# A batched matmul on one core: half of the last group's x moved to GpSimd's DMA queue

## The chip, the cores and the metric

The kernel runs on one core of a Trainium2 chip. The core has five engines with an instruction stream each (TensorE or PE, VectorE or DVE, ScalarE or ACT, GpSimd or POOL, SyncE or SP) and sixteen DMA engines that they share. The metric is the device time of one execution in microseconds (us), lower is better. A run of the kernel before took 517.88 us (median of three, 517.79 to 517.91).

## What is computed

```python
def setup_inputs():
    b1, b2, m, k, n = 8, 16, 256, 512, 384
    return {
        "x": np.random.randn(b1, b2, m, k).astype(np.float32),
        "weight": np.random.randn(b1, b2, k, n).astype(np.float32),
    }

def reference(x, weight):
    return np.matmul(x, weight).astype(np.float32)
```

These are 128 products of a 256x512 by a 512x384 matrix: x has 67.1 MB, weight 100.7 MB, the output 50.3 MB, 218 MB in all, each moved once.

## The kernel before

**Tiling.** The 128 batches are taken in NG = 32 groups of G = 4. One group has 1024 rows of x. They lie in SBUF as 128 partitions of R = 8 rows, 16 KB for a partition, 2 MB in all. Its w has 3 MB, its output 1.5 MB. In groups 0 to 30 a partition holds eight consecutive rows of x, so a partition belongs to one batch, and the multiplication is done with 32 columns at a time for each batch. In the last group, n = 31 (`is_full`, L123), x is laid out by batch instead: a partition holds two consecutive rows of each of the four batches, four runs of 4 KB, and each batch is multiplied at the full width of 128 (`multiply_full`, L251).

**Stages.** For each group, x is loaded as float32 (`load_x`, L108), cast to bf16 by DVE in T = 4 pieces of two rows (`cast_x`, L164; the line of the copy in the profile is L171), transposed by PE in pairs of bf16 taken as float32 words (`transpose`, L216, L224), copied out of PSUM by ACT (`evacuate`, L205, L211) and multiplied (`multiply`, L231, L242; the last group L260). w is loaded (`load_w`, L126), cast to bf16 by DVE and ACT (`cast_w`, L176, L184), or by DVE alone in the first four and the last two groups (`cast_short`, L189, L200), for which w also comes in two halves with a semaphore each (`h_in`). ACT copies the products from PSUM to SBUF (`copy_out`, L269, L275), and they are stored (`store`, L142, L157). In the last group, piece q of x, of its cast and of its product is batch q of the four.

**Buffers and order.** x and w have two buffers each (XS, WS), the output four. The order on each engine is written out by hand, and semaphores count the pieces. Every load and store is issued by SyncE, which runs through them in the order x of n + 4, store of n, w of n + 4, and waits in front of each until its buffer is free or its data are there. For x of group n that is `x_cast` reaching (n - 1) * 4, that is, the cast of group n - 2 wholly done (L111): group 29 for group 31. Since SyncE waits in order, a load stands behind the wait of the one before it. Its last issues are: x of 30, store of 26, w of 30 in halves, x of 31, w of 31 in halves, the stores of groups 27 to 30, and the store of 31, in a layout by batch as its x (L145, L154). Then SyncE waits for the stores, with a short loop and some semaphore increments between (L305 to L310).

**DVE's order** in a step n is: cast w of group n, cast x of group n + 1 (`next_x`, L315). In the last steps this makes: w of 29, x of 30, w of 29 (rest), w of 30, x of 31, w of 31. `cast_x` waits for the load once, ahead of its first piece (L166, L167).

**GpSimd** makes the identity matrix for the transposes at the start (`on_gpsimd`, L280) and has no further work until the closing barrier.

**DMA semaphores.** A transfer adds 16 to its semaphore. The trace has sixteen increments of one for every transfer, each at its own time, one for each DMA engine.

## Time and profile before

| | us |
|---|---|
| median of three runs | 517.88 |
| the profiled execution | 517.57 |
| its span in the profile | 515.80 |
| PE busy (matmul) | 320.0 (62%) |
| DVE busy | 397.7 (77%) |
| ACT busy | 409.7 (79%) |
| POOL busy | 0.7 |

The span runs from the first to the last instruction; the execution is 1.77 us longer. 218.18 MB were moved at a mean of 423 GB/s. The parts of the profile used here are: the page with its forty equal slices (a digit is a busy share in tenths), the table of stretches (busy time of each engine, granted clock, mean busy share of the sixteen DMA engines, GB/s), the chain of work that ended last (start, duration, what), and the timeline (start, duration, engine, line, operation, out<-in, and in brackets how long the engine stood idle before it and for whom).

SyncE's last issues, from the timeline: w of 30 at 464.46 (both halves, 0.80 us), x of 31 at 465.32 (0.42 us), w of 31 at 480.32 (0.81 us), the stores from 481.23 on, the last at 506.13. From issue to landing, x took 22.3 us in the median, a store 25.0 us, a half of w 16.7 us.

### The profile page before, as it was taken

The page shows a single profiled execution, that of the slowest core. Times are in us where ns is not written, and L with a number is a line of the kernel's source. Part 1 is how long each engine was busy: PE and PEld are TensorE (multiplying, and loading weights), DVE is VectorE, ACT ScalarE, POOL GpSimd, SP SyncE. Part 2 cuts the span into 40 slices and gives each one's busy share as a digit, 9 for nine tenths or more (in the row PEclk, how much of TensorE's full clock was granted, in tenths as well). Part 3 has the DMA queues.
Part 4 walks back from the last instruction along what each step waited for, and adds up shares of the span by engine and source line. Part 5 has one row for each costly group of instructions (what it writes and reads, how often), then busy time and mean ns, then how long its engine had stood idle before and what let it go on. Part 6 is the DMA issues. An engine that isn't in the chain of part 4 may idle for free.

```text
span 515.8 us, 11659 instructions
## 1 busy us (share of the span) xinstructions
PE 320.0 (62%) x4512; PEld 222.0 (43%) x4512; DVE 397.7 (77%) x462; ACT 409.7 (79%) x387; POOL 0.7 (0%) x6
## 2 busy tenths in 40 slices
PE   2276737567586656675655864767657477656871
PEld 2254425444354443453443543535445354434550
DVE  2788757788777897777977778877789777797960
ACT  1365577798978997987998799889798978997751
POOL 0000000000000000000000000000000000000000
PEclk9698878677866877876888686778667876877697
DMA  8999999999999999999999999999999999999996
GB/s 337 428 423 426 437 430 420 435 431 433 431 424 432 430 439 428 429 426 432 433 436 428 423 434 431 437 429 425 430 431 434 433 429 427 430 435 423 421 429 250
DMA packets 15462, 218.18 MB, mean 423 GB/s; under 512 B 1632, under 2 KB 1632, under 8 KB 2656
## 3 DMA queue, kind: packets, MB, share of 16 engines
q1 hardware_dynamic: 15456, 218.11, 99.3%
q8 instruction: 3, 0.05, 0.0%
q14 instruction: 3, 0.02, 0.0%
HBM read 167.77 MB, written 50.33 MB: 423 GB/s over the span
## 4 chain that ended last, share of the span: by engine, by line
DMA 57%; DVE 29%; issue 9%; PE 1%; DVEq 1%; SPq 1%; ACT 0%; POOLq 0%
DMA w_sb<-in_weight_dram 57%; DVE w_bf L184 20%; DVE x_bf L171 5%; DVE w_bf L200 4%; PE po L260 1%; SPq L135 0%; DVEq L334 0%; SPq L118 0%; DVEq L62 0%; DVEq L180 0%; ACT out_sb L275 0%; SPq L130 0%; DVEq L168 0%; DVEq L194 0%; SPq L422 0%
## 5 line engine op out<-in xcount | busy, mean ns | idle before, releaser
L184 DVE CAST w_bf<-w_sb 32x1536 bf16<-32x1536 f32 x286 | 271.9, 951 | 81.1 <-DMA w_sb<-in_weight_dram 73.0
L242 PE MATMUL po<-w_bf,x_t 128*32 128x384 bf16 x3968 | 201.5, 364 | 33.4 <-DVE w_bf L184 25.4
L224 PE MATMUL pt<-identity,x_bf 128*128 128x128 f32 x512 | 113.5, 409 | 149.1 <-DVE x_bf L171 149.1
L184 ACT CAST w_bf<-w_sb 32x1536 bf16<-32x1536 f32 x130 | 191.0, 1470 | 5.1 <-DMA w_sb<-in_weight_dram 1.9
L224 PEld LDWEIGHTS pt<-identity,x_bf 128*128 128x128 f32 x512 | 101.3, 223 | 161.5 <-issue 161.0
L242 PEld LDWEIGHTS po<-w_bf,x_t 128*32 128x32 bf16 x3968 | 117.7, 107 | 116.3 <-issue 51.5
L275 ACT COPY out_sb<-po 128x768 f32 (+1 forms) x128 | 102.5, 800 | 59.7 <-PE po L242 53.9
L211 ACT COPY x_t<-pt 128x1024 bf16<-128x1024 bf16 x128 | 123.6, 1021 | 20.9 <-PE pt L224 20.3
L171 DVE CAST x_bf<-x_sb 128x1024 bf16<-128x1024 f32 x128 | 80.0, 688 | 12.5 <-DMA x_sb<-in_x_dram 11.7
L200 DVE CAST w_bf<-w_sb 64x1536 bf16<-64x1536 f32 x48 | 45.8, 955 | 8.3 <-DMA w_sb<-in_weight_dram 7.0
L211 ACT ACT_TABLE_LOAD x1 | 1.3, 1283 | 10.8 <-PE pt L224 10.8
L260 PE MATMUL po<-w_bf,x_t 128*128 128x384 bf16 x32 | 5.4, 326 | 2.8 <-DVE w_bf L200 2.8
L260 PEld LDWEIGHTS po<-w_bf,x_t 128*128 128x128 bf16 x32 | 3.1, 98 | 5.1 <-issue 3.1
masks.py:199 POOL TENSOR_SCALAR_AFFINE_SELECT identity<-identity 128x128 f32<-128x128 f32 x1 | 0.3, 294 | 0.2 <-POOL identity L281 0.2
L281 POOL MEMSET identity<- 128x128 f32 x1 | 0.2, 205 | 0.5 <-POOLq L62 0.5
L411 POOL MEMSET const-bfloat16-1.0<- 128x1 bf16 x1 | 0.1, 102 | 0.0
L411 POOL MEMSET const-uint8-127<- 128x1 uint8 x1 | 0.1, 102 | 0.0
L411 POOL MEMSET const-float32-0.0<- 128x1 f32 x1 | 0.1, 99 | 0.2 <-issue 0.2
L411 POOL MEMSET const-float32-1.0<- 128x1 f32 x1 | 0.1, 99 | 0.0
## 6 DMA issues: line engine op xcount, KB each, us to landing
w_sb<-in_weight_dram SPq DMA_DIRECT2D x26, 3072.0 KB, 18.2
x_sb<-in_x_dram SPq DMA_DIRECT2D x32, 2048.0 KB, 22.3
out_dram<-out_sb SPq DMA_DIRECT2D x32, 1536.0 KB, 25.0
w_sb<-in_weight_dram SPq DMA_DIRECT2D x12, 1536.0 KB, 16.7
```

What stands on the lines that cost most here:

```text
L171: e.tensor_copy(out=x_bf[s % BS][:, rows].rearrange("p r (s q c) -> p r s q c", s=S, c=KO), in_=x_sb[s % XS][:, rows].rearrange("p r (q s ...
L184: copy(out=w_bf[(s * G + i) % WBS][h * C : (h + 1) * C], in_=w_sb[s % WS][i * C : (i + 1) * C, h * KO : (h + 1) * KO, :],).then_inc(w_vcas ...
L200: e.tensor_copy(out=w_bf[(n * G + d * SH + a) % WBS][h * p : (h + 1) * p], in_=w_sb[n % WS][a * p : (a + 1) * p, r : r + KO, :],).then_inc ...
L211: e.copy(out=x_t[s % TS][:, 2 * q : 2 * q + 2], in_=pt[(s * T + q) % PT][:].bitcast(bf16),).then_inc(t_copied, 1)
L224: ins = e.transpose(pt[(s * T + q) % PT][:, rr, h, :], words[:, 2 * q + rr, h :: KO // 2], identity[:],)
L242: ins = e.matmul(po[(s * T + q) % PO][mine, rr, :N], x_t[s % TS][:, 2 * q + rr, ko // 2, mine, ko % 2], w_bf[(s * G + i) % WBS][:, ko, :], ...
L260: ins = e.matmul(po[(s * T + q) % PO][:, rr, :N], x_t[s % TS][:, 2 * q + rr, ko // 2, :, ko % 2], w_bf[(s * G + q) % WBS][:, ko, :], start ...
L275: e.copy(out=out_sb[:, bass.ds(slot(t, U, s) * R + 2 * q, 2), :], in_=po[(s * T + q) % PO][:, :, :N],).then_inc(o_copied, 1)
L281: e.memset(identity[:], 0.0).then_inc(id_done, 1)
L411: nc = _bacc.Bacc("TRN2", target_bir_lowering=False, num_devices=1)
```

## The change

GpSimd gets a function `load_rest`. After the identity it waits for the same count of `x_cast` that SyncE waits for ahead of x of group 31, resets the cursor of its DMA descriptors, and issues the loads of batches 2 and 3 of that group (the pieces `G // 2 :` of each partition, two runs of 4 KB, 1 MB in all) as three transfers of 5, 121 and 2 partitions, on a semaphore of their own (`rest_in`). SyncE's load of group 31 is cut to batches 0 and 1, 1 MB, at its old place. DVE's cast of that group waits for `rest_in` to reach 48 ahead of its third piece (q = 2), the first that reads the other half.

```diff
+    rest_in = sems("rest_in", 1)[0]
...
         rows = x_rows[bass.ds(n * (G * M), G * M)]
         if is_full(n):
-            src = rows.rearrange("(i p r) k -> p i r k", i=G, p=P)
-            dst = x_sb[s % XS][:].rearrange("p (i r) k -> p i r k", i=G)
+            src, dst = (v[:, : G // 2] for v in full_x())
         else:
             src, dst = rows.rearrange("(p r) k -> p r k", r=R), x_sb[s % XS][:]
         e.dma_start(dst, src).then_inc(x_in[s % XS], 16)
+
+    def full_x():
+        n = NG - 1
+        src = x_rows[n * G * M : (n + 1) * G * M].rearrange("(i p r) k -> p i r k", i=G, p=P)
+        return src, x_sb[n % XS][:].rearrange("p (i r) k -> p i r k", i=G)
+
+    def load_rest(e):
+        n = NG - 1
+        e.wait_ge(x_cast, n * T + (1 - XS) * T)
+        e.inc_swdge_sem([], [], mode="reset_dge_cursor")
+        src, dst = full_x()
+        p = 0
+        for k in (5, 121, 2):
+            e.dma_start(dst[p : p + k, G // 2 :], src[p : p + k, G // 2 :]).then_inc(rest_in, 16)
+            p += k
...
         if q == 0:
             e.wait_ge(x_in[s % XS], (t * (U // XS) + s // XS) * 16 + 16)
+        if q == T // 2 and is_full(n):
+            e.wait_ge(rest_in, 16 * 3)
         e.wait_ge(t_made, n * T + (q + 1 - T + BIAS))
...
         e.drain().then_inc(id_done, 1)
+        load_rest(e)
```

## The prediction

> **What bounds the kernel now.** I read the transfers' view first, since the page has DVE at 77% and ACT at 79% of the span and PE at 62%, and none of them full. Page, slices and queues:

> ```profile
> DMA  8999999999999999999999999999999999999996
> ...
> GB/s 337 428 423 426 437 430 420 435 431 433 431 424 432 430 439 428 429 426 432 433 436 428 423 434 431 437 429 425 430 431 434 433 429 427 430 435 423 421 429 250
> ...
> q1 hardware_dynamic: 15456, 218.11, 99.3%
> ```

> Only the first and last slice fall below 420 GB/s. The sixteen DMA engines are the bound, all on SyncE's queue, and transfers wait in it: the last x was issued at 465.32 and landed at 487.99. So time can only come from the two ends. The end, by stretches of 1 us (last two columns: mean busy share of the sixteen, GB/s):

> ```profile
> 506.00:507.00 1.00, 0.00 (x0) 0.00 (x0) 0.00 (x0) 0.11 (x1) 0.00 (x0) 1.00 0.50 209
> 507.00:508.00 1.00, 0.00 (x0) 0.00 (x0) 0.00 (x0) 0.00 (x0) 0.00 (x0) 1.00 0.97 393
> ...
> 511.00:512.00 1.00, 0.00 (x0) 0.00 (x0) 0.00 (x0) 0.00 (x0) 0.00 (x0) 0.50 0.23 89
> 512.00:513.00 1.00, 0.00 (x0) 0.00 (x0) 0.00 (x0) 0.00 (x0) 0.00 (x0) 0.50 0.07 28
> 513.00:514.00 1.00, 0.00 (x0) 0.00 (x0) 0.00 (x0) 0.00 (x0) 0.00 (x0) 0.50 0.07 27
> ```

> 0.07 is one engine in sixteen (0.0625): from 512.2 on a single DMA engine works, and in 506:507 half of them have nothing to do. They end unequally. The records of each transfer's sixteen semaphore increments, one for each DMA engine, say by how much (us behind the first, 11th to 16th; the records are in order of time and don't name the engine):

> ```
> transfer, landed      11th  12th  13th  14th  15th  16th
> first w,      12.42   0.37  0.38  0.43  0.55  0.66  0.73
> next w half,  17.23   0.37  0.41  0.54  0.65  0.71  1.84
> w, group 3,   50.41   0.53  0.64  0.72  1.63  1.69  1.90
> w, second to last half, 491.69   1.03 1.33 1.89 1.98 2.45 3.60
> w, last half, 495.36  1.01  1.32  1.87  1.95  2.42  3.58
> store of 30, 510.46   1.02  1.33  1.91  1.99  2.44  4.11
> store of 31, 514.54   0.12  0.19  0.63  0.73  1.17  3.22
> ```

> Eleven lie within 1.02 us, five straggle by up to 4.1. The stragglers are made partly by instruction fetches: three packets of 16 KB on the instruction queue (15.2, 35.0 and 43.5 us, about 1.03 to 1.1 us each) precede the three steps of about 1 us in the table.

> The chain of waits breaks off at the last ACT copy. Its last lines, with SyncE's and DVE's:

> ```profile
> 480.32 11.37 DMA w_sb<-in_weight_dram
> ...
> 499.91 5.37 PE po L260 x32
> 505.29 0.02 issue
> 505.31 0.80 ACT out_sb L275
> ```

> ```profile
> 458.99 2.50 DVE L171 CAST x_bf<-x_sb 128x1024 bf16<-128x1024 f32 x4
> 461.52 2.91 DVE L184 CAST w_bf<-w_sb 32x1536 bf16<-32x1536 f32 x3
> 466.99 7.83 DVE L184 CAST w_bf<-w_sb 32x1536 bf16<-32x1536 f32 x8 [2.55 <-DMA w_sb<-in_weight_dram]
> ...
> 488.21 2.50 DVE L171 CAST x_bf<-x_sb 128x1024 bf16<-128x1024 f32 x4
> 491.81 7.86 DVE L200 CAST w_bf<-w_sb 64x1536 bf16<-64x1536 f32 x8 [1.09 <-DMA w_sb<-in_weight_dram]
> ```

> The last store is issued at 506.13 and its engines without backlog finish together near 511.35: that is the floor which the compute chain sets, 5.2 us after the issue. The end, 514.54, lies 3.2 us above it, on one DMA engine which was still busy with store 30. So the end is backlog of the slowest DMA engine, not the chain.

> **The change, part by part.** *Prices.* x of group 31 goes in packets of 4 KB, four for a partition: between the landings of the w before it (482.92) and its own (487.99) lie 5.07 us for 8 partitions per engine, 0.158 us a packet and 0.317 us for a partition's half. Store 31 takes an engine that starts late 3.70 us (13th to 15th: 508.26 to 511.95, 508.34 to 512.05, 508.79 to 512.49); the 16th took 4.08, with an 8 KB instruction packet of 0.31 us at 513.79 behind its data.

> *SyncE.* Its one x issue (0.42 us) stays, at half the bytes; nothing leaves its queue.

> *GpSimd.* One wait, one cursor reset, three issues, none of them in the trace of before. The wait is met when the casts of group 29 end, 461.49, which is 3.8 us ahead of SyncE's issue, and these packets needn't stand behind SyncE's backlog. Behind them on POOL stands only the closing barrier (from 499.75). The cost of an issue is bounded below by SyncE's 0.33 us, above by a whole landing time, 22.7 us; I take the low end, SyncE's issue being the nearest row, so about 1.3 us for the four, and with the 0.9 us from issue to first packet seen at store 31 (506.13 to 507.06) the rest starts near 464. The third cast of x, which now waits for it, starts at 489.46. At any price up to about 20 us this is hidden under DVE's work until then; without that cover each us goes onto DVE's chain. Starting early gains nothing by itself: the DMA share is 0.98 at 460 to 464, so early bytes displace others.

> *DVE.* One more semaphore check, 0.05 us by the like step at 491.71; the chain has 3.2 us of room.

> *Who carries the bytes.* 128 partitions went eight to an engine, as the equal times per engine show. If transfers of 5, 121 and 2 partitions split into equal whole shares, only 5x1, 11x11 and 2x1 spread them: five engines carry one partition (two of these a second one), eleven carry eleven. Eleven engines gain 3 x 0.317 = +0.95 us, three lose 7 x 0.317 = -2.22, two lose 6 x 0.317 = -1.90. The trace has eleven punctual engines and five late ones; if the light five are the late five, ends become:
> - slowest: 510.46 - 2.22 + 4.08 = 512.32 (512.64 with two partitions; 511.94 without the fetch's 0.38)
> - 11th, the last punctual one: 506.35 + 1.02 + 0.95 + 3.70 = 512.02
> - floor: 511.35, or lower.

> So 514.54 becomes 512.32: -2.22 us.

> *The order.* Ahead of w of group 30 now lie eleven partitions (3.49 us) on punctual engines: its halves land at 475.58 + 1.02 + 3.49 = 480.09 and 479.28 + 1.03 + 3.49 = 483.80, where DVE wants them at 480.32 and, four casts of 0.98 on, 484.24. Hidden by 0.2 to 0.4; if not, DVE slips by as much, inside its room. Later all is earlier: x and w of group 31 land 1.6 us sooner, w's casts start behind x's at 490.71 instead of 491.81, the last store goes out 1.1 us sooner. That only lowers the floor.

> The profiled execution took 517.57 (span 515.80): 517.57 - 2.22 = 515.35. The median, 517.88, lies 0.31 above it: **515.7**. Own range 515.1 (no fetch at the end, 0.2 of play) to 516.4 (two partitions on the slowest, and 0.4 for GpSimd's unseen costs).

> **Rivals.** A measurement of this kernel tells 0.2%, 1.04 us, from no change.

> *B, the light five aren't the late five.* The slowest takes eleven: 514.54 + 0.95 = 515.49, **518.8**. Its w of 30 comes 3.5 us later, but that chain, worked through, ends at a floor of 512.6. For it: the records name no engine, so the match rests on two counts of five. Against: three fetches made three different engines late, as if each instruction stream had an engine of its own, and there are five streams. [...] No row here numbers the engines.

> *C, it doesn't do what it says.* Sixteen nearly equal shares come out, 8 or so for most and one engine light: 514.54 plus 0 to 2 x 0.317, **517.9 to 518.5**; if the light one is the slowest, the 15th decides, 512.49 plus 0 to 0.63, 515.8 to 516.5. For it: every transfer of before was spread so; against: 121 has no such equal split. [...]

> *D, GpSimd is held up by DVE's casts.* DVE idles 464.43 to 466.99 and then hardly until 489.46, where it would stop for the rest. If nothing is written out while it casts and the idle 2.55 us don't suffice, the rest starts there: 1.2 for three issues, 0.9 to the first packet, 11 x 0.317 = 3.5, doubled as the stores' packets alternate, gives 498.6; two casts (1.25), eight of w (7.86), 0.24 and PE's 5.37, the copy and issue 0.83, and 5.22 to the landing: 519.4, that is **522.7**. Landing after 491.5 costs, after about 494 more than the balance brings. For it: DVE's back-to-back rows; against: 28 us and a gap. [...]

> **Chances.** A 0.58, B 0.18, C 0.14, D with its milder forms 0.10. Faster by over 0.2%: A and 0.04 of C, 0.62. Same: 0.10 of C and, as 518.8 lies just inside 518.92, 0.11 of B: 0.21. Slower: 0.07 of B and D: 0.17. The range 515.1 to 518.9 holds A, C and two thirds of B, a little over 0.8.

> **What would show it.** Right: the transfers' view has a second queue with about 1 MB; in the last stretches the share falls from near 1 to 0 within 2 us, with no run of 0.07; store 30 lands between 505.5 (light engines) and 508.3, a spread of 2.9 at most. The queue's packets should start near 464, DVE's third cast of x should not wait, and SyncE's last store should go out near 505.0. Wrong: a lag above 4.5 at store 30 (B), lags as before (C), or DVE idle at 489.5 (D).

## The result, and the profile after

The changed kernel takes 520.51 us (median of 6, 520.24 to 520.81), the kernel before, run beside it, 517.66 (517.32 to 517.91): a ratio of 1.0055, 95% interval 1.0042 to 1.0068. It is slower by 2.8 us where 2.2 us less were forecast. Its profiled execution took 520.48, its span is 518.7.

The transfers' view of the page: slices and queues.

```profile
DMA  8999999999999999999999999999999999999996
GB/s 334 432 423 428 430 431 421 432 431 432 435 425 426 433 435 435 428 425 432 433 435 425 428 431 431 433 434 429 423 432 431 440 429 428 425 434 360 373 427 274
...
q1 hardware_dynamic: 15200, 217.06, 98.8%
q0 software_dynamic: 464, 1.05, 0.6%
```

GpSimd's megabyte is there, on its own queue. Two slices (467 to 493 us) fall from about 430 to 360 and 373 GB/s, and the DMA digits above them stay at 9: the engines were busy all the time and moved less. GpSimd issued its three transfers early, as meant:

```profile
462.33 3.00 POOL L132 DMA_DIRECT2D x_sb<-in_x_dram  x3 [460.61 <-DVE x_bf L188]
```

The same loss in stretches around the new transfers (last three columns: granted clock of PE, mean busy share of the sixteen DMA engines, GB/s). Before:

```profile
466.00:470.00 4.00, 4.00 (x84) 2.27 (x76) 2.92 (x4) 2.33 (x3) 0.00 (x0) 0.77 0.98 416
470.00:474.00 4.00, 1.73 (x40) 0.88 (x32) 3.88 (x5) 3.93 (x5) 0.00 (x0) 1.00 1.03 438
474.00:484.00 10.00, 7.16 (x60) 5.25 (x64) 9.75 (x12) 8.47 (x8) 0.00 (x0) 0.53 1.00 416
```

After:

```profile
466.00:470.00 4.00, 3.87 (x96) 2.40 (x90) 2.77 (x3) 3.94 (x5) 0.00 (x0) 1.00 1.01 384
470.00:474.00 4.00, 0.54 (x16) 0.12 (x4) 3.87 (x5) 3.93 (x5) 0.00 (x0) 0.93 1.01 398
474.00:484.00 10.00, 6.97 (x64) 5.23 (x68) 6.32 (x9) 7.12 (x7) 0.00 (x0) 0.51 1.01 308
```

Taken over 466 to 486 the mean is 348 GB/s against 423 before: 20 us x 75 GB/s = 1.5 MB less, which is 3.5 us of all sixteen engines at 423 GB/s. In the packets' records SyncE's 12 KB packets of 474 to 484 take 644 ns in the mean (462 before), GpSimd's 4 KB packets 191 ns in the mean of all, half of those there 200 to 250 (0.158 us in the prediction's sum). From 470 to 474, where SyncE's queue carries the store of group 26, the usual packet takes 460 and 159 ns (78 of 95 of SyncE's 12 KB packets 465 or less, 71 of 76 of GpSimd's 162 or less): beside this store most are undisturbed, beside the load at 474 to 484 they aren't.

The timeline of DVE. Before, its casts of w of group 30 began without a wait:

```profile
480.32 7.86 DVE L200 CAST w_bf<-w_sb 64x1536 bf16<-64x1536 f32 x8
```

After:

```profile
477.56 2.91 DVE L201 CAST w_bf<-w_sb 32x1536 bf16<-32x1536 f32 x3
484.92 7.87 DVE L217 CAST w_bf<-w_sb 64x1536 bf16<-64x1536 f32 x8 [4.45 <-DMA w_sb<-in_weight_dram]
492.81 2.50 DVE L188 CAST x_bf<-x_sb 128x1024 bf16<-128x1024 f32 x4
495.23 7.86 DVE L217 CAST w_bf<-w_sb 64x1536 bf16<-64x1536 f32 x8
```

and, of the chain that ended last, the load of w of 30 and the end:

```profile
464.55 20.24 DMA w_sb<-in_weight_dram
...
503.33 5.38 PE po L277 x32
508.70 0.02 issue
508.73 0.80 ACT out_sb L292
```

w of group 30 lands at 484.80, not 480.09, DVE idles 4.45 us in front of it, and the chain ends 3.4 us later than before (ACT's last copy at 508.73, not 505.31). So there are two candidates for the loss: the late chain, or the DMA engines' lost time. The last stretches and the landings:

```profile
514.00:515.00 1.00, 0.00 (x0) 0.00 (x0) 0.00 (x0) 0.00 (x0) 0.00 (x0) 0.50 0.61 240
515.00:516.00 1.00, 0.00 (x0) 0.00 (x0) 0.00 (x0) 0.00 (x0) 0.00 (x0) 0.50 0.25 101
516.00:517.00 1.00, 0.00 (x0) 0.00 (x0) 0.00 (x0) 0.00 (x0) 0.00 (x0) 0.50 0.06 24
```

```
after: transfer, landed   sixteen lags behind the first landing, us
w of 29,          467.08  0 .02 .09 .15 .32 .34 .48 .58 .77 .85 1.05 1.16 | 2.10 2.40 2.71 3.64
w of 31 2nd half, 498.29  0 .37 .83 1.01 | 1.94 2.04 2.22 2.24 2.40 2.53 2.60 2.85 | 3.65 3.94 4.11 4.28
store of 31,      517.20  0 .01 .01 .02 .02 .07 .08 .09 .10 .11 .12 | .50 1.53 1.70 1.88 2.46
```

The bars stand at the larger gaps between the sixteen. Eleven engines end at the new floor (514.74 to 514.86), the slowest at 517.20, still with backlog: its landings from w of 31 on follow each other in 3.5 to 4.0 us. Behind the same bytes as before it is already late at w of 31, 498.29 against 495.36, ahead of the stores that the late chain could hold up.

### The profile page after: what moved, and what is told of

Its sections match the earlier page's. It is cut to its first block, busy times and chain, and to the rows that moved or that the text cites. A ratio compares the mean times of both kernels' runs of the same rounds, so it can differ in the third digit from the quotient of the medians.

```text
span 518.7 us, 11664 instructions
## 1 busy us (share of the span) xinstructions
PE 315.3 (61%) x4512; PEld 222.2 (43%) x4512; DVE 397.6 (77%) x462; ACT 409.6 (79%) x387; POOL 3.7 (1%) x9
## 2 busy tenths in 40 slices
DMA  8999999999999999999999999999999999999996
## 3 DMA queue, kind: packets, MB, share of 16 engines
q0 software_dynamic: 464, 1.05, 0.6%
## 4 chain that ended last, share of the span: by engine, by line
DMA 57%; DVE 30%; issue 9%; PE 1%; SPq 0%; DVEq 0%; ACT 0%; POOLq 0%
DMA w_sb<-in_weight_dram 57%; DVE w_bf L201 20%; DVE x_bf L188 5%; DVE w_bf L217 5%; PE po L277 1%; SPq L150 0%; DVEq L185 0%; DVEq L62 0%; ACT out_sb L292 0%; SPq L145 0%; SPq L118 0%; DVEq L211 0%; SPq L440 0%; POOLq L62 0%; DVEq L197 0%
## 5 line engine op out<-in xcount | busy, mean ns | idle before, releaser
L259 PE MATMUL po<-w_bf,x_t 128*32 128x384 bf16 x3968 | 195.0, 355 | 34.2 <-DVE w_bf L201 20.5
L241 PE MATMUL pt<-identity,x_bf 128*128 128x128 f32 x512 | 115.2, 416 | 158.8 <-DVE x_bf L188 158.8
L241 PEld LDWEIGHTS pt<-identity,x_bf 128*128 128x128 f32 x512 | 103.9, 225 | 170.6 <-issue 170.5
L259 PEld LDWEIGHTS po<-w_bf,x_t 128*32 128x32 bf16 x3968 | 115.2, 104 | 112.8 <-issue 48.8
L132 POOL DMA_DIRECT2D x_sb<-in_x_dram x3 | 3.0, 1003 | 460.6 <-DVE x_bf L188 460.6
```

The source lines that it names most:

```text
L132: e.dma_start(dst[p : p + k, G // 2 :], src[p : p + k, G // 2 :]).then_inc(rest_in, 16)
L241: ins = e.transpose(pt[(s * T + q) % PT][:, rr, h, :], words[:, 2 * q + rr, h :: KO // 2], identity[:],)
L259: ins = e.matmul(po[(s * T + q) % PO][mine, rr, :N], x_t[s % TS][:, 2 * q + rr, ko // 2, mine, ko % 2], w_bf[(s * G + i) % WBS][:, ko, :], ...
```

## The experiments

Three theories stood against each other. P: the odd transfers make DMA engines write partitions that other engines are writing for SyncE's loads, and both are held up. S: GpSimd's queue disturbs the other whatever the shape. H: two loads in flight disturb each other's reads in HBM, the memory that x, w and the output lie in. A fourth question was whether the light five (the engines with one or two of GpSimd's partitions) are the late five.

**One transfer of 128 partitions instead of three (the even run).**

```diff
-        for k in (5, 121, 2):
+        for k in (128,):
...
-            e.wait_ge(rest_in, 16 * 3)
+            e.wait_ge(rest_in, 16)
```

> The same early load from GpSimd, but as one transfer of 128 partitions instead of 5, 121 and 2. Theory P (the odd transfer makes a DMA engine write into partitions that another engine is writing for SyncE's load, and both are slowed): each engine stays with its own eight partitions, so the w packets of group 30 stay at 460 ns, the GpSimd packets at 159 ns, no dip in GB/s between 468 and 486 us; eight partitions (2.53 us) still stand ahead of w of group 30, which lands at 481.7 instead of 484.8, DVE waits 1.4 us there, and the time is 517.7 (517.2 to 518.3). Theory S (packets of GpSimd's queue slow the other queue whatever their shape): packets of w at 600 to 700 ns as in the changed kernel, w of 30 near 484, time 520 to 521. Theory H (two loads in flight at once disturb each other in reading HBM): as S.

Measured: 517.99 against 517.77, ratio 1.0006 (0.9997 to 1.0015). The same stretches, in this run:

```profile
466.00:470.00 4.00, 3.87 (x96) 2.42 (x92) 3.05 (x4) 3.46 (x4) 0.00 (x0) 1.00 0.99 416
470.00:474.00 4.00, 0.56 (x16) 0.13 (x7) 3.88 (x5) 3.93 (x5) 0.00 (x0) 1.00 1.03 433
474.00:484.00 10.00, 7.29 (x64) 5.43 (x68) 8.23 (x11) 7.45 (x8) 0.00 (x0) 0.50 1.00 420
```

```profile
481.74 7.86 DVE L217 CAST w_bf<-w_sb 64x1536 bf16<-64x1536 f32 x8 [1.58 <-DMA w_sb<-in_weight_dram]
```

The dip is gone: GpSimd's packets take 159 ns, SyncE's 460, and DVE waits 1.58 us for w where 1.4 were expected. The early issue, GpSimd's queue and a second load in flight cost nothing that this run can tell (ratio 1.0006): S and H fall.

**The order 121, 5, 2.**

```diff
-        for k in (5, 121, 2):
+        for k in (121, 5, 2):
```

> The three transfers in the order 121, 5, 2 after the reset, so that other engines should be the light ones. If the light five of the changed kernel are the late five, the late ones now carry 10 partitions more (3.2 us) and the last landing comes up to 3 us later: 521.5 to 524, with a larger spread of the landings of store 30 than 3.9 us. If the changed kernel relieved the wrong engines (rival B), the spread shrinks and the time is 518.5 to 520. If the bytes are spread evenly in both (rival C), time and spread are those of the changed kernel, 520.5 and 3.9 us. Theories P, S and H all expect the dip in GB/s here too.

Measured: 521.20, ratio 1.0072 (1.0057 to 1.0087), with the dip (358 GB/s over 466 to 486, 348 in the changed kernel). It is below the range of the first case, outside that of rival B, and 0.7 us above that of rival C. The slowest engine's landing of w of 31 is the telling number: 498.30 here, 498.29 in the changed kernel. Other engines should be light here; the records don't name them, but the sixteen landings of that transfer now spread over 5.69 us instead of 4.28, so the shares lie elsewhere. The last landing has moved by a hundredth of a us, where ten partitions more on the slowest engine should have been 3.2 us. As far as one profile each can tell, it isn't which engine carries GpSimd's bytes that sets that landing. Which engines were relieved this run doesn't say.

**The megabyte left out.**

```diff
-        load_rest(e)
...
-        if q == T // 2 and is_full(n):
-            e.wait_ge(rest_in, 16 * 3)
```

> SyncE loads its half of x of group 31 and nobody loads the other (batches 2 and 3 of that group are computed from what was in the buffer; DVE doesn't wait for them). What the MB costs by itself when nothing else changes: 1.05 MB at 430 GB/s is 2.4 us on the DMA engines. If the end is the backlog of the slowest DMA engine: 517.7 - 2.5 = 515.2, and the last landing about 512.1. If the chain through w of 30, x and w of 31 were the bound: w of 31 lands 2.5 us earlier, its casts start 1.1 us earlier, 516.6.

Measured: 517.00 (516.16 to 517.46), ratio 0.9984 (0.9975 to 0.9994): a gain of 0.8 us, neither 2.5 nor 1.2. The stretches of the profiled execution (517.27) show where some of the rest went:

```profile
486.00:488.00 2.00, 1.42 (x36) 0.73 (x31) 1.94 (x3) 1.33 (x2) 0.00 (x0) 1.00 1.04 369
488.00:490.00 2.00, 0.98 (x7) 0.95 (x8) 1.97 (x4) 0.41 (x2) 0.00 (x0) 1.00 1.06 227
490.00:492.00 2.00, 2.00 (x11) 1.65 (x10) 1.97 (x4) 2.00 (x3) 0.00 (x0) 0.62 0.86 313
```

While w of 31 is loaded the rate falls to 227 GB/s at a full busy share (424 before), without any packet of GpSimd. SyncE's 12 KB packets of 488 to 490 take 912 ns in the mean. Why is open, as is whether the quicker executions (down to 516.16) had it too, and so this run puts no price on the megabyte.

**Transfers by themselves.** No compute; each case waits for the one before. The plan, as what SyncE moves, who moves the half of x, and in which parts:

```diff
+        ("w", None, ()),
+        (None, "pool", (121,)),
+        (None, "pool", (5, 121, 2)),
+        (None, "pool", (128,)),
+        ("w", "pool", (121,)),
+        ("w", "pool", (128,)),
+        ("w", "act", (128,)),
+        ("w", "act", (121,)),
+        ("o", "pool", (121,)),
+        ("w", "pool", (5, 121, 2)),
```

> Nothing is computed: transfers alone, one case after the other, each waiting for the one before. SyncE's w (3 MB, 24 KB for a partition, some 912 ns a packet) or a 1.5 MB store, beside GpSimd's or ACT's half of x as 121 or as 128 partitions. P expects: 121 partitions alone land on eleven engines after the time of 22 packets (3.5 us or more), the five others add their increments at once; 121 beside the w load: w packets well over 912 ns from GpSimd and from ACT alike; 128 beside the w load: 912 and 159 ns from both; 121 beside the store: undisturbed. S expects GpSimd's 121 and 128 beside w both slow, ACT's both undisturbed. H expects all four beside w slow. If the 121 go to sixteen engines evenly, all sixteen increments come together and rival C's split is what the chip does.

```
case                     4 KB packets, mean ns   24 KB packets of w, mean ns
w alone                          -                       974
GpSimd 121 alone                265                       -
GpSimd 5, 121, 2 alone          275                       -
GpSimd 128 alone                166                       -
GpSimd 121 beside w             257                     1101
GpSimd 128 beside w             159                     1012
ACT 128 beside w                160                      997
ACT 121 beside w                230                     1153
GpSimd 5, 121, 2 beside w       275                     1044
```

Alone, 121 partitions land five increments at 13.66 to 13.75 us and eleven at 19.85 to 20.35: five engines without data, and for the other eleven eleven partitions each (242 packets of 4 KB). The 121 split as I worked out, and rival C falls. The rest is P: beside w 121 partitions are slow from GpSimd's queue and from ACT's, and 128 are not, from either. The 121 slow themselves too, without any other load (GpSimd's alone): 22 packets took 6.6 us (13.28 to 19.91), not 3.5. In the last row of the table GpSimd's packets came when half of w was through (111.87 of 107.64 to 115.96). The store case tells nothing, since GpSimd's first packet (99.84) came when the store was nearly done.

**64 + 64 partitions: equal shares, other partitions.**

```diff
-        for k in (5, 121, 2):
+        for k in (64, 64):
...
-            e.wait_ge(rest_in, 16 * 3)
+            e.wait_ge(rest_in, 32)
```

> GpSimd's half as two transfers of 64 partitions: every DMA engine gets eight partitions in all, as in the even run, but four at a time, so they are no longer the eight that it carries in SyncE's loads. P (the partition an engine writes decides, not how many it has): a dip in GB/s and w packets well over 460 ns as in the changed kernel, w of 30 lands 2 to 4 us later than in the even run (481.7), time 519 to 521. If unequal shares are what costs (eleven engines with eleven partitions), nothing of that: as the even run, 518.0.

Measured: 520.54, ratio 1.0049 (1.0035 to 1.0063). The transfers' view of 456 to 519 us, in forty slices:

```profile
GB/s 429 476 390 453 416 411 406 294 307 322 398 414 385 346 341 416 414 414 398 453 421 440 414 453 406 429 429 421 437 406 453 414 453 211 164 398 400 123 29 0
```

The dip is back with equal shares, down to 294, and so is the time of the changed kernel. Unequal shares aren't the cause; of the two things that this run was to tell apart, which partitions an engine writes is left. (Nor is it that there are two transfers instead of one: the single one of 121 was slow in the run above.)

**Which engines are the light five.** The kernel before, with a mark:

```diff
+    marked = sems("marked", 1)[0]
+    scratch = sbuf("scratch", [32, 3072], fp32, 1)[0]
...
+        e.wait_ge(x_cast, 24 * T)
+        for j in range(8):
+            e.inc_swdge_sem([], [], mode="reset_dge_cursor")
+            e.dma_start(
+                scratch[0:20:4, :],
+                x_rows[j * 32 : j * 32 + 30].rearrange("(p r) k -> p (r k)", r=6),
+            ).then_inc(marked, 16)
+            e.wait_ge(marked, 16 * j + 16)
```

> The kernel before, with eight extra transfers from GpSimd around 400 us: after a cursor reset, 12 KB to each of the partitions 0, 4, 8, 12 and 16 of an unused buffer. They keep the five engines that a transfer of 5 gets after a reset busy for 8 x 0.46 = 3.7 us. If these are the five late engines (my forecast), the five last of the sixteen landings of every later transfer move back by 3.7 us against the other eleven, and the end comes up to 3.7 us later, 521. If they are others (rival B), five of the eleven punctual ones move back and land with or after the late ones, the slowest stays, and the time grows by 0 to 1 us.

Measured: 522.53 (two executions) against 517.84, ratio 1.0091 (1.0073 to 1.011): 4.7 us slower, more than either case had. All forty packets took 460 to 474 ns, 3.7 us for each of five engines. The landings of w before and after the mark:

```
at 371.66   0 .08 .16 .22 .28 .28 .36 .47 .56 .61 .96 1.20 | 2.03 2.48 2.58 3.02
at 438.85   0 .09 .15 .20 .20 .29 .42 .53 | 1.96 2.42 2.51 | 3.55 4.12 4.50 4.76 6.82
```

Three late engines stay (2.03, 2.48, 2.58 against 1.96, 2.42, 2.51). The slowest moves, 3.02 to 6.82, and with it four of the punctual ones: 0, 0.56, 0.96 and 1.20 plus about 3.6 give 3.55, 4.12, 4.50 and 4.76. The five engines of the mark are the slowest and four punctual ones, as far as the equal shifts tell; the one at 1.20 is the twelfth, which the prediction had still counted among the late five. The changed kernel's table fits: behind GpSimd's transfers, at w of 31, four engines lead the next by 0.9 us. If these five are the ones that the 121 leave out, three of the late engines were among the eleven that got more: my forecast and rival B were each right in part.

**Eight engines, partitions side by side or apart.**

```diff
...
+        (None, "sync", "in", (0, 1)),
+        (None, "sync", "in", (0, 4)),
+        (None, "sync", "in", (0, 16)),
+        (None, "pool", "in", (0, 1)),
+        (None, "pool", "in", (0, 4)),
+        (None, "sync", "out", (0, 1)),
+        (None, "sync", "out", (0, 4)),
+        (None, "pool", "halves", ()),
+        ("w", "pool", "halves", ()),
```

> Transfers alone again, nothing computed. Eight partitions of 16 KB, one for each of eight engines, to partitions 0 to 7 side by side, to every fourth and to every sixteenth; from SyncE and from GpSimd; then the same as stores; then 64 + 64 partitions of the half of x, alone and beside w. P expects: every fourth partition at the usual 612 ns a packet; side by side slower, up to four times (2.4 us) if four neighbouring partitions share one way into SBUF; the same from SyncE and GpSimd; 64 + 64 slower than 128 at 166 ns a packet, and w beside it above its 1012 ns beside 128. If only queues or shares mattered, all eight-partition cases are alike at 612 ns.

As loads it tells little: 0.81 to 1.33 us a packet side by side, 0.87 to 1.08 apart, from both queues; all eight read neighbouring rows, one packet each. As stores it is clear: every fourth partition 460 to 462 ns, side by side 1546 to 1858 ns, up to four times. 64 + 64 take 318 ns for a 4 KB packet alone and 269 beside w, whose packets take 1202 ns in the mean; with one transfer of 128 these were 166, 159 and 1012 in the run above.

**Single packets from far rows.**

```diff
+        far = x_rows[: count * 1008].rearrange("(p r) k -> p r k", r=1008)[:, :R]
+        e.dma_start(x_sb[0][p : p + (count - 1) * by + 1 : by], far)
```

> Transfers alone, nothing computed: 16 KB to each of 8, 4 or 2 partitions, one DMA engine each, from rows of x that lie 2 MB apart, so that the reads can't be in each other's way; only the partitions written differ. P expects 612 ns a packet wherever every engine writes a group of four partitions of its own (spacing 4), and longer ones side by side: for 4 and 8 partitions side by side up to four times, for 2 less. If the reads in HBM were what slowed the odd transfers, all cases are alike at 612 ns.

Measured: 0.6 to 1.6 us a packet over all cases, with no order in them. The run decides nothing: single packets from neighbouring rows were as mixed (0.81 to 1.33 us), and one packet for an engine is no test. The next run has more packets.

**Five packets in a row.**

```diff
+    plan = [(8, 4), (8, 1), (4, 4), (4, 1), (2, 4), (2, 1), (2, 32), (16, 4), (16, 1)]
...
+        for c, place in enumerate(places):
+            far = x_rows[c * 16 : c * 16 + count * 1008].rearrange("(p r) k -> p r k", r=1008)[:, :R]
+            nc.sync.dma_start(place[0 : (count - 1) * by + 1 : by], far).then_inc(done, 16)
```

> As the run before with single packets, whose 0.9 to 1.0 us each are mostly the first packet's way, so it told little: now five packets of 16 KB in a row on each of 2 to 16 engines, read 2 MB apart, and only the partitions written differ. From the second packet on, P expects 612 ns where each engine has a group of four partitions to itself (spacing 4), and clearly more where engines write side by side into one group (spacing 1), for 4 engines more than for 2. If HBM's side were the cause, all cases are alike.

```
engines, spacing of partitions    the most frequent time of a 16 KB packet, ns
 4, 4 and 2, 4                      611
 8, 4                               611 (a third of them; the others 640 to 1490)
 2, 1 (neighbours)                 1285
 2, 32                             1285
16, 4 (partitions 0 to 60)         1285
 4, 1                              2430 to 2500
 8, 1 and 16, 1                    2400 to 2415
```

**Is it the late chain?** The even run, with three more casts on DVE, one ahead of each of the first three of w of 30:

```diff
+    twice = sbuf("twice", [P, KO, N], bf16, 3)
...
+                    if n == NG - 2 and c < 3:
+                        e.tensor_copy(
+                            out=twice[c][h * p : (h + 1) * p],
+                            in_=w_sb[n % WS][a * p : (a + 1) * p, r : r + KO, :],
+                        )
```

> The even run, with three extra casts (into an unused buffer) ahead of the casts of w of group 30 on DVE, 2.93 us, so that the chain through w of 30, x and w of 31 runs as late as in the changed kernel (the last store issued near 509.4 there and here), while no DMA packet is slowed. If the changed kernel is slower because of DVE's wait for w of group 30, this run is as slow: 520.5. If it is slower because its DMA engines lost time, the late chain only lifts the floor, 509.4 + 5.25 = 514.7, to where the slowest DMA engine ends anyway (514.8): 518.0 to 518.4.

Measured: 518.23, ratio 1.0008 (0.9999 to 1.0017), with the chain nearly as late as in the changed kernel:

```profile
508.39 0.80 ACT L298 COPY out_sb<-po 128x768 f32<-128x768 f32 x1 [0.50 <-PE po L283]
```

The store of 31 landed on all sixteen engines within 0.47 us, the last at 514.89. A chain 3 us late was absorbed by the slack above the floor. What the changed kernel has beyond this run are its slowed packets (644 and 191 ns in the mean), so the 2.8 us are the DMA engines' lost time.

## Why the prediction was wrong, point by point

**What bounds the end** was right: backlog of the slowest DMA engine, with some 3 us of room for the chain, as the late-chain run shows.

**GpSimd's start** was mis-sized without consequence. An issue takes 1.0 us, not 0.33, and from the end of DVE's casts to the first packet 5.2 us pass (461.58 to 466.81; I had 2.2), 4.5 of them behind the start of the first issue. With no DVE at work and w beside it, these were 4.5 us as well (36.92 to 41.47), with idle queues 1.7 (11.62 to 13.28). So rival D doesn't show, and DVE's third cast of x never waited. The three issues did take 3.00 us beside DVE's casts and 1.97 without them, in the run of transfers by themselves; the 1.03 us between are about one cast of w (0.95), so a delay of a cast or so isn't excluded. D's sum doubled a time because packets of the two queues were to alternate on an engine; that was an estimate, and no run shows it packet by packet. From 474 to 484 there are 142 of GpSimd's 4 KB packets and 202 of SyncE's 12 KB packets over the sixteen engines.

**Who carries the bytes** is the step that failed, in its price. The split of the 121 over eleven engines was right. That the three transfers take turns, so that the five of the first (and the two of the last) are engines which the 121 leave out, was my assumption: no run shows the turn itself; shown are the eleven and five of the 121 alone, five engines moved by a transfer of 5, and the four that lead by 0.9 us at w of 31. But 0.317 us for a partition's half is the price of two packets of a transfer over 128 partitions, in which, by the inference above, an engine writes into its own eight, and the step put it on packets that it writes into another's. One engine's load, 12 KB in 460 ns or 26.7 GB/s, is about what the way into a group took in the run of five packets (26.8), so I read the longer packets as GpSimd's and SyncE's waiting for each other there: 191 ns instead of 159, 644 instead of 462. Where the step took 2.22 us off the slowest engine, the last landing of w of 31 came 2.9 us later than before (498.29 against 495.36). The relief may have failed in the same way: a light engine's partitions still get their bytes through the same way, whoever sends them, so their owner's load queues there. That would explain why the order of the three transfers left the slowest landing at 498.3; no run shows it by itself.

**Which engines are relieved** was half right, if the light engines are the five of the mark. The count of five late engines was weak already: only 0.3 us lay between the eleventh and the twelfth (1.02 and 1.33). The store of 30, which should have landed within 2.9 us, took 3.9 (509.27 to 513.16), less than the 4.5 that would have spoken for B. At undisturbed prices, with the slowest relieved and three late ones loaded, the 15th would have decided: 508.79 + 0.95 + 3.70 = 513.44, so 1.1 us to be had and not 2.2. Measured is 517.20. The 3.8 us between are near the 3.5 us that the engines lost by the GB/s; that the whole difference is this is worked out, not shown by a run of its own. The mean over sixteen engines is a rough measure, too: with 64 + 64 partitions the same sum gives 2.3 us (374 GB/s over 466 to 486), and its slowest landing of w of 31 was as late (498.61).

**The order** was right in kind: w of 30 is pushed back. In the even run, with eight partitions ahead of it, it came as the same kind of sum had it (forecast 481.7, landed 481.62, DVE's wait 1.58); in the changed kernel it came 4.7 us later than forecast, through the slowed packets, and that cost nothing at the end.

**The rivals.** B held for three of the late engines. C and D fell. The one that fits the runs, engines meeting on the way into SBUF (16 KB in 1285 ns for two on neighbouring partitions, 611 for one), wasn't among them, although the row that all my prices rest on, equal times for equal shares, was a transfer over 128 partitions and said nothing of another spread.

## What to carry to other kernels

A DMA engine's bandwidth wasn't the only limit of a transfer here: four neighbouring partitions had one as well, 26 to 27 GB/s with four engines on them. In the transfers over all 128 partitions here 4 KB packets took 166 ns alone; in those over 121 and 64 + 64 they took 265 and 318. Before work is moved from one DMA engine to another, ask through whose partitions it goes: here an odd split, most of it beside a load, took 3.5 us from the sixteen engines in the mean, more than the 2.2 us that it was to give back to the late one. To find out what a full busy share hides, put GB/s and the packets' durations beside it.

## What the runs showed of the hardware that was not expected

- Side by side, two engines on neighbouring partitions take 1285 ns for a 16 KB packet, four 2430 to 2500, in loads; in stores 12 KB take up to 1858 ns against 460. Four neighbouring partitions pass about what one DMA engine delivers to one, 26 to 27 GB/s against 26.8.
- Most packets written into SBUF by GpSimd's transfers beside SyncE's store out of it weren't slowed (159 and 460 ns at 470 to 474; 71 of 76 and 78 of 95 packets).
- With SyncE's queue full, GpSimd's first packet comes 3.9 to 4.7 us after its issue begins (462.54 to 466.40 with 64 + 64 partitions, 53.54 to 58.21 beside w alone); ACT's came 3.3 us after (65.61 to 68.95).
- With a megabyte less to load, w of 31 ran at 227 GB/s for 2 us at a full busy share. Its cause stays open.
